# Attention by runs of two pairs of blocks, with TensorE in program order inside the loop

## The chip, the cores and the metric

The kernel runs on one core of one Trainium2 chip (trn2). The metric is the device time of one execution in microseconds. Other times are from one profiled execution of the kernel before.

## The reference

One hybrid decoder block over 2048 tokens of width 1024, batch 1, depth 1. One input projection gives an LRU branch, its gate, and q, k, v; a recurrence (RG-LRU) and a sliding-window attention run side by side; their normed outputs go through one output projection; a squared-ReLU MLP follows. What the change touches is the attention (16 query heads of 64, 2 key/value heads, blocks of 128 queries against the block before and their own, a learned sink in the denominator):

```python
def sliding_window_sink_attention(q, k, v, sinks):
    ...
    scores = jnp.einsum('bnqhgd,bnkhd->bnhgqk', qb, kwin).astype(jnp.float32) * scale
    ...
    mask = (kpos <= qpos) & (kpos > qpos - WINDOW) & (kpos >= 0)
    scores = jnp.where(mask[None, :, None, None], scores, NEG_INF)
    ...
    m = jnp.maximum(jnp.max(scores, axis=-1, keepdims=True), sink)
    p = jnp.exp(scores - m)
    denom = jnp.sum(p, axis=-1, keepdims=True) + jnp.exp(sink - m)
    probs = (p / denom).astype(v.dtype)
    out = jnp.einsum('bnhgqk,bnkhd->bnqhgd', probs, vwin)
```

## The kernel before

The sequence is worked in two halves of 1024 tokens (`c` = 0, 1; eight blocks of 128 each). A half goes through the norm and its transposes, the projections of k and v, the attention loop, the LRU, the output projection and the first MLP product; the second MLP product comes after both halves. Float32 factors are split into a high and a low part (`split_weight`, L157 to L168: `whi` on ScalarE at L166, `wlo` on VectorE at L167), so a projection is three matmuls (L224, L225, L227).

**The attention loop** (`for s in range(NH + 1)`, NH = 16 heads) is a software pipeline. Step `s` computes the scores of head `s`, the transposed probabilities of head `s - 1` and, four pairs later, the value products; beside them it runs pieces of a projection. It goes over four pairs of blocks, `p` = 0 to 3. What one pair issues:

- `Head.scores`: four matmuls (L584, tile `sc`) into one PSUM bank, two of which take turns; VectorE selects the window (L592, or L589 and L590 at the first pair of the first half), takes the maximum (L594) and scales it (L595); ScalarE does two exponentials into `st` (L598).
- `Head.probs`: two transposes (L614) into `tpb[:, p % 2]`; ScalarE copies them out as the high half of `pf` (L617), VectorE makes the low half (L618), GpSimd selects the two windows (L621, L623).
- `Head.values`: twelve matmuls of 64 columns (L638, tile `av`) from `pf`. Behind the fourth pair VectorE scales the head's result (L645, `yq`).
- `piece`: six matmuls of 512 columns, of the next q projection (`qps`), and near the end of the loop of the LRU's first inputs (`xps`, `gpps`). When a q projection is done, at the end of every even step, it is scaled and split: ScalarE L562 and VectorE L563, twice.
- `flip`, once in two heads: eight transposes (L655, `ytp`), ScalarE's copy L656 and square L662, VectorE's L665.

Both halves of `tpb` are one tile of 2 KB per partition, in one PSUM bank:

```python
tpb = bank(2, "tp", (P, 2, 2, P))
...
tp = tpb[:, p % 2]
```

**What sets the order.** The framework orders the instructions of each engine itself, by a priority heap over the traced program and a model of its own, and puts in the waits on semaphores. Each engine then issues its list strictly in that order. The change names TensorE as an engine whose list is the program's own, between two points.

Of the kernel before, what the change touches and what calls it, by code (L numbers as in the profile page):

```python
# [37 lines left out]
def hybrid_block_kernel(  # L38
# [16 lines left out]
    act = nc.scalar  # L55
    dve = nc.vector
    pe = nc.tensor
    chain = [None]

    def chained(ins):  # L60
# [24 lines left out]
    def U(i, name, dt=F32, shape=(P, D)):  # L85
        return S(f"u{i}", name, dt, shape)
# [400 lines left out]
    for c in range(NCH):  # L487
# [59 lines left out]
        def new_q(j):  # L547

            w = split_weight(w_in[16 + j])
            ps = mm("qps", j % 2)  # L550

            def piece(i):
                n, k = divmod(i, 4)
                proj_mm((ps[:, :HALF], ps[:, HALF:]), w, hn, (n,), (2 * k, 2 * k + 1))

            def done():

                qs = [U((16, 8, 9, 10)[(2 * j + hh) % 4], "qs", F32R) for hh in range(2)]
                for hh in range(2):
                    s_ = slice(hh * HD, hh * HD + HD)  # L560
                    o_ = slice((1 - hh) * HD, (1 - hh) * HD + HD)
                    act.activation(qs[hh][s_, :], ps[s_, :], AF.Copy, scale=0.125)  # L562
                    dve.scalar_tensor_tensor(out=qs[hh][o_, :], in0=ps[s_, :], scalar=0.125,  # L563
                                             in1=f32(qs[hh][s_, :]), op0=ALU.mult, op1=ALU.subtract)
                return qs
            return piece, done
# [83 lines left out]
        def flip(j, yq):  # L650

            yt = U(15, "yt")
            tp = mm("ytp", j % 2)
            for b in range(NT):
                pe.transpose(tp[:, b * P:(b + 1) * P], yq[:, b, :], ident)  # L655
            act.activation(yt, tp, AF.Copy, scale=usc[:, j // 4:j // 4 + 1])  # L656
            nc.gpsimd.dma_start(ydr[j], yt)
            if j == 0:
                act.activation(acca, yt, AF.Square)
            else:  # L660
                sq = yq.rearrange("p a b -> p (a b)")
                act.activation(sq, yt, AF.Square)  # L662
                for m in range(2):
                    hs = slice(m * HALF, (m + 1) * HALF)
                    dve.tensor_tensor(acca[:, hs], acca[:, hs], sq[:, hs], op=ALU.add)  # L665
# [77 lines left out]
        qs, yqs, heads = {}, {}, {}  # L743
        pf_next = [0]
        late = []
        piece, done = new_q(0)
# [3 lines left out]
        piece, done = new_q(1)  # L750
        for i in range(4):
            piece(i)
        lru_in = None
        for s in range(NH + 1):
            j = s // 2
            if s < NH:
                if s % 2 == 0:
                    yqs[j] = U(3 + j % 2, "yq", F32, (P, NT, P))
                heads[s] = Head(s, qs[j][s % 2], yqs[j])
            if s % 2 == 1:  # L760
                if j + 2 < KT:
                    piece, done = new_q(j + 2)
                else:
                    piece, done = (new_x if j + 2 == KT else new_gate)(0)
            for p in range(4):
                if s < NH:
                    heads[s].scores(p)
                    if p == 3:
                        heads[s].sums()
                if len(late) == 4:  # L770
                    for _ in range(2):
                        heads[late[0][0]].values(late.pop(0)[1])
                if s > 0:
                    heads[s - 1].probs(p)
                    late.append((s - 1, p))
                    if p == 3 and s % 2 == 1 and s > 1:
                        flip(j - 1, yqs[j - 1])
                piece(p if s % 2 else 4 + p)
            if s % 2 == 0:
                if j + 1 < KT:  # L780
                    qs[j + 1] = done()
                elif j + 1 == KT:
                    lru_in = done()
                else:
                    lru_in.append(done())
        for h, p in late:
            heads[h].values(p)
        flip(KT - 1, yqs[KT - 1])
# [450 lines left out]
```

## Time and profile before

| | |
|---|---|
| median of 3 runs | 2533.41 us (2530.89 to 2533.82) |
| the profiled execution | 2528.75 us |
| its span | 2527.0 us |
| TensorE busy in the span | 2427.9 us, 96% |
| VectorE, ScalarE, GpSimd | 70%, 50%, 19% |
| attention loop of the first half, first scores of head 0 to those of head 15 | 70.56 to 229.34 us |
| the same of the second half | 1000.16 to 1159.08 us |

A row of the timeline has the start, the time from the first start to the last end of the merged instructions, the engine, the source line and operation, the tiles (out<-in), the shapes and the count; in brackets the engine's idle time just before and what ended it. Matmuls overlap, so what one costs is read from start to start.

### The profile page before, as it was taken

What the parts mean: (1) busy time and instruction counts of PE and PEld (TensorE: products, weight loads), DVE (VectorE), ACT (ScalarE), POOL (GpSimd) and SP (SyncE); (2) the same over time, 40 slices, a digit from 0 to 9 for tenths busy, and PEclk for the clock granted to TensorE, in tenths of its full rate; (3) what the DMA queues carried; (4) which work ended last, traced back from release to release, by engine and by line L of the source; (5) the groups of instructions that cost most, each with busy time, mean ns of one, the idle gap of its engine ahead of it and who ended that gap; (6) DMA issues with size and microseconds to landing.
All of it is one profiled execution on the core that took longest, in us unless ns stands there. A gap on an engine that the chain in (4) does not pass through costs nothing.

```text
span 2527.0 us, 32551 instructions
## 1 busy us (share of the span) xinstructions
PE 2427.9 (96%) x12338; PEld 1981.7 (78%) x12338; DVE 1768.6 (70%) x2389; ACT 1253.8 (50%) x2084; POOL 481.7 (19%) x461
## 2 busy tenths in 40 slices
PE   7999999999999999999999998999989999999997
PEld 6887787787788877887778787788868777888885
DVE  6788566857655565876758748555575898887888
ACT  5666777414554465666778215454454233222334
POOL 0355000001333210554000011233230110111100
PEclk9999999999999999999999999999989999999999
DMA  4111112312344443111114212444453454443334
GB/s 154 43 51 43 53 45 101 120 50 105 112 151 156 147 167 117 42 48 51 45 44 141 101 42 92 146 146 154 150 200 117 154 162 156 134 136 119 127 103 148
DMA packets 133324, 276.37 MB, mean 109 GB/s; under 512 B 11184, under 2 KB 70576, under 8 KB 133168
## 3 DMA queue, kind: packets, MB, share of 16 engines
q1 hardware_dynamic: 125680, 248.08, 29.2%
q0 software_dynamic: 4608, 16.78, 1.8%
q10 hardware_dynamic: 2880, 9.44, 0.9%
q8 instruction: 97, 1.59, 0.2%
q14 instruction: 59, 0.48, 0.1%
HBM read 190.37 MB, written 83.89 MB: 109 GB/s over the span
## 4 chain that ended last, share of the span: by engine, by line
PE 63%; DVE 16%; issue 12%; ACT 7%; POOL 1%; DMA 1%; POOLq 0%; SPq 0%; DVEq 0%; ACTq 0%
PE ops L932 11%; PE dd L1149 10%; PE qr L394 10%; PE pa L394 9%; PE pb L394 3%; PE sc L584 2%; DVE acc L1158 2%; PE qps L224 2%; PE qps L227 2%; PE qps L225 2%; DVE xc L691 2%; PE xps L225 1%; PE xps L224 1%; PE xps L227 1%; PE av L638 1%
## 5 line engine op out<-in xcount | busy, mean ns | idle before, releaser
L1158 DVE TENSOR_TENSOR acc<-dd,acc 128x1024 f32<-128x1024 f32 x207 | 250.9, 1219 | 94.1 <-PE dd L1149 93.5
L932 PE MATMUL ops<-whi,ht 128*128 128x512 f32 x1024 | 277.6, 390 | 0.0
L962 ACT ACTIVATE ah<-araw 128x1024 fp32r<-128x1024 f32 x96 | 101.9, 1061 | 293.4 <-PE dd L1149 284.8
L932 PEld LDWEIGHTS ops<-whi,ht 128*128 128x128 f32 x1024 | 192.2, 188 | 40.7 <-DVE x L937 0.5
L932 PE MATMUL ops<-wlo,ht 128*128 128x512 f32 x512 | 159.7, 391 | 0.0
L372 POOL TENSOR_TENSOR s<-wraw 128x512 f32<-128x512 f32 x32 | 42.0, 1313 | 598.9 <-issue 327.8
L166 ACT ACTIVATE whi<-wraw 128x1024 fp32r<-128x1024 f32 x84 | 88.6, 1056 | 121.5 <-PE ops L932 92.6
L621 POOL TENSOR_SCALAR_AFFINE_SELECT pf<-pf 128x512 f16<-128x512 f16 x128 | 86.1, 673 | 315.3 <-DVE pf L618 314.7
L963 DVE TENSOR_TENSOR al<-araw,ah 128x1024 fp32r<-128x1024 f32 x96 | 123.1, 1284 | 11.6 <-ACT ah L962 11.5
L598 ACT ACTIVATE st<-sc,mx 128x128 f32<-128x128 f32 x256 | 91.6, 364 | 63.1 <-DVE mx L595 62.6
L167 DVE TENSOR_TENSOR wlo<-wraw,whi 128x1024 fp32r<-128x1024 f32 x82 | 104.4, 1278 | 25.5 <-issue 9.8
L932 PEld LDWEIGHTS ops<-wlo,ht 128*128 128x128 f32 x512 | 95.6, 188 | 20.5 <-DVE wlo L167 1.2
L224 PE MATMUL qps<-ht,whi 128*128 128x512 f32 x256 | 108.3, 423 | 0.0
L380 ACT ACTIVATE f2h<-wraw 128x1024 fp32r<-128x1024 f32 x32 | 34.0, 1061 | 142.9 <-DMA act<-hid 111.9
L394 PE MATMUL qr<-hm,s 128*128 128x512 f32 x384 | 100.3, 411 | 3.6 <-DVE hid L427 3.6
L225 PE MATMUL qps<-ht,whi 128*128 128x512 f32 x256 | 102.0, 398 | 0.0
L224 PE MATMUL xps<-ht,whi 128*128 128x512 f32 x256 | 101.5, 396 | 0.0
L227 PE MATMUL qps<-ht,wlo 128*128 128x512 f32 x256 | 101.2, 395 | 0.0
L225 PE MATMUL xps<-ht,whi 128*128 128x512 f32 x256 | 100.9, 394 | 0.0
L224 PE MATMUL gpps<-ht,whi 128*128 128x512 f32 x256 | 100.8, 394 | 0.0
L225 PE MATMUL gpps<-ht,whi 128*128 128x512 f32 x256 | 100.1, 391 | 0.0
L381 DVE TENSOR_TENSOR f2l<-wraw,f2h 128x1024 fp32r<-128x1024 f32 x32 | 39.2, 1224 | 79.4 <-ACT f2h L380 79.4
(324 smaller groups left out, 6899.6 us busy)
## 6 DMA issues: line engine op xcount, KB each, us to landing
araw<-act SPq DMA_DIRECT2D x96, 512.0 KB, 3.5
wraw<-in_w_up_dram SPq DMA_DIRECT2D x64, 512.0 KB, 3.2
act<-hid SPq DMA_DIRECT2D x128, 256.0 KB, 2.6
wraw<-in_w_in_dram SPq DMA_DIRECT2D x52, 512.0 KB, 3.2
act<-a SPq DMA_DIRECT2D x96, 256.0 KB, 2.4
wraw<-in_w_out_dram SPq DMA_DIRECT2D x32, 512.0 KB, 3.2
braw<-in_w_down_dram SPq DMA_DIRECT2D x32, 512.0 KB, 4.3
xt<-in_x_dram SPq DMA_DIRECT2D x16, 512.0 KB, 4.5
```

The source lines that it names most:

```text
L166: act.activation(hi, raw, AF.Copy)
L167: (eng or dve).tensor_tensor(lo, raw, f32(hi), op=ALU.subtract)
L224: pe.matmul(ps[m], w[0][:, k * P:(k + 1) * P], hk(ht[m][0], k), start=(k == 0), stop=False)
L225: pe.matmul(ps[m], w[0][:, k * P:(k + 1) * P], hk(ht[m][1], k), start=False, stop=False)
L227: pe.matmul(ps[m], w[1][:, k * P:(k + 1) * P], hk(ht[m][0], k), start=False, stop=(k == KT - 1))
L394: pe.matmul(ps, w[a_][:, ks], hk(h[b_], k), start=first and k == 0 and i == 0, stop=k == KT // 2 - 1 and i == 2, skip_group_check=True)
L598: ins = act.activation(self.st[:, b, :], cur[:, i, :], AF.Exp, bias=self.mx[:, b:b + 1], accum_out=self.ls[:, b:b + 1])
L932: pe.matmul(ps[m], a_, wk[k][b_][:, hs], start=(k == 0 and a_ is yh and b_ == 0), stop=(k == kn - 1 and a_ is ylo))
L962: act.activation(hi, raw, AF.Copy)
L963: dve.tensor_tensor(lo, raw, f32(hi), op=ALU.subtract)
L1149: pe.matmul(o[:, i, :], a_[:, t0:t0 + P], b_[:, r, :], start=first and r == 0 and k == 0, stop=r == 1 and k == 2, skip_group_check=True)
L1158: dve.tensor_tensor(accs[blk][d_], o, accs[blk][d_], op=ALU.add)
```

## The change

The loop body takes the four pairs in two runs (`p0` = 0 and 2). A run issues the scores of two pairs, then the value products of two pairs, then the transposes of two pairs, then two pieces of a projection. Around the loop, `tc.manual_schedule(engines={PE})` keeps TensorE's instructions in the order in which the program issues them; the other engines are ordered by the framework as before.

```diff
--- before.py
+++ after.py
@@ -55,6 +55,7 @@
     act = nc.scalar
     dve = nc.vector
     pe = nc.tensor
+    PE = mybir.EngineType.PE
     chain = [None]
 
     def chained(ins):
@@ -751,6 +752,8 @@
         for i in range(4):
             piece(i)
         lru_in = None
+        order = ctx.enter_context(ExitStack())
+        order.enter_context(tc.manual_schedule(engines={PE}))
         for s in range(NH + 1):
             j = s // 2
             if s < NH:
@@ -762,20 +765,24 @@
                     piece, done = new_q(j + 2)
                 else:
                     piece, done = (new_x if j + 2 == KT else new_gate)(0)
-            for p in range(4):
+
+            for p0 in (0, 2):
                 if s < NH:
-                    heads[s].scores(p)
-                    if p == 3:
+                    for p in (p0, p0 + 1):
+                        heads[s].scores(p)
+                    if p0:
                         heads[s].sums()
                 if len(late) == 4:
                     for _ in range(2):
                         heads[late[0][0]].values(late.pop(0)[1])
                 if s > 0:
-                    heads[s - 1].probs(p)
-                    late.append((s - 1, p))
-                    if p == 3 and s % 2 == 1 and s > 1:
+                    for p in (p0, p0 + 1):
+                        heads[s - 1].probs(p)
+                        late.append((s - 1, p))
+                    if p0 and s % 2 == 1 and s > 1:
                         flip(j - 1, yqs[j - 1])
-                piece(p if s % 2 else 4 + p)
+                for p in (p0, p0 + 1):
+                    piece(p if s % 2 else 4 + p)
             if s % 2 == 0:
                 if j + 1 < KT:
                     qs[j + 1] = done()
@@ -783,6 +790,7 @@
                     lru_in = done()
                 else:
                     lru_in.append(done())
+        order.close()
         for h, p in late:
             heads[h].values(p)
         flip(KT - 1, yqs[KT - 1])
```

Line numbers behind the inserted lines are one higher in the changed kernel up to the loop (L618 becomes L619, L614 becomes L615), and eight higher behind it.

TensorE at step 1, where the first transposes of the loop stand, in the kernel before (`kcar` and `kd` are keys, `tp` the transposes, `qps` the projection; the names in brackets are the semaphores waited for, DVE is VectorE):

```order
L584 MATMUL sc<-kcar,qs 128x256 [waits DVE_49,PE_49,Activation_49]
L584 MATMUL sc<-kcar,qs 128x256
L584 MATMUL sc<-kd,qs 128x256 x2
L614 MATMUL tp<-ident,st 128x128 x2
L224 MATMUL qps<-ht,whi 128x512
L225 MATMUL qps<-ht,whi 128x512
L227 MATMUL qps<-ht,wlo 128x512
L224 MATMUL qps<-ht,whi 128x512
L225 MATMUL qps<-ht,whi 128x512
L227 MATMUL qps<-ht,wlo 128x512
L584 MATMUL sc<-kd,qs 128x256 [waits DVE_49,PE_49,Activation_49]
L584 MATMUL sc<-kd,qs 128x256 x3
```

The same place in the changed kernel:

```order
L585 MATMUL sc<-kcar,qs 128x256 [waits DVE_49,PE_49,Activation_49]
L585 MATMUL sc<-kcar,qs 128x256
L585 MATMUL sc<-kd,qs 128x256 x2
L585 MATMUL sc<-kd,qs 128x256 [waits DVE_49,PE_49,Activation_49]
L585 MATMUL sc<-kd,qs 128x256 x3
L615 MATMUL tp<-ident,st 128x128 x2
L615 MATMUL tp<-ident,st 128x128 [waits DVE_49]
L615 MATMUL tp<-ident,st 128x128
L225 MATMUL qps<-ht,whi 128x512
L226 MATMUL qps<-ht,whi 128x512
L228 MATMUL qps<-ht,wlo 128x512
```

The first two transposes carry no wait in either; the next two, which stood behind projections and scores, now stand right behind the first two, with a wait for VectorE.

VectorE at the beginning of step 5, an odd step, in the kernel before (`wlo` is the low part of a weight, `mx` the maximum of scores, `pf` the transposed probabilities):

```order
L167 TENSOR_TENSOR wlo<-wraw,whi 128x1024
L606 TENSOR_TENSOR ls<-ls,es 128x8
L589 COPY_PREDICATED sc<-prevm,negt 128x128
L607 TENSOR_SCALAR ls<-ls 128x8
L590 COPY_PREDICATED sc<-prevm,sc 128x128
L608 RECIPROCAL ls<-ls 128x8
L594 TENSOR_REDUCE mx<-sc 128x2
L563 SCALAR_TENSOR_TENSOR qs<-qps,qs 64x1024
L595 TENSOR_SCALAR mx<-mx,snk 128x2
L618 SCALAR_TENSOR_TENSOR pf<-tp,pf 128x256
L592 COPY_PREDICATED sc<-prevm,sc 128x2x128
```

And in the changed kernel:

```order
L168 TENSOR_TENSOR wlo<-wraw,whi 128x1024
L590 COPY_PREDICATED sc<-prevm,negt 128x128
L564 SCALAR_TENSOR_TENSOR qs<-qps,qs 64x1024
L591 COPY_PREDICATED sc<-prevm,sc 128x128
L593 COPY_PREDICATED sc<-prevm,sc 128x2x128
L595 TENSOR_REDUCE mx<-sc 128x2 x2
L564 SCALAR_TENSOR_TENSOR qs<-qps,qs 64x1024
L596 TENSOR_SCALAR mx<-mx,snk 128x2 x2
L619 SCALAR_TENSOR_TENSOR pf<-tp,pf 128x256 x2
```

Before, one of the two `qs` operations stood ahead of the first `pf` of the step; now both do, and the work on two tiles of scores.

## Rows read from the trace of the kernel before

**Rows 1.** The page's first part: busy us, share of the span and instructions by engine

```profile
PE 2427.9 (96%) x12338; PEld 1981.7 (78%) x12338; DVE 1768.6 (70%) x2389; ACT 1253.8 (50%) x2084; POOL 481.7 (19%) x461
```

**Rows 2.** Stretches of the span: length, busy us and count by engine, clock, DMA

```profile
70.56:229.34 158.78, 153.37 (x1385) 130.49 (x1384) 128.14 (x338) 101.27 (x342) 76.74 (x117) 1.00 0.12 44
```

**Rows 3.** TensorE's timeline, two pairs of blocks in step 2

```profile
91.95 0.64 PE L584 MATMUL sc<-kd,qs 128*128 128x256 f32 x4
92.43 0.26 PE L638 MATMUL av<-vpa,pf 128*128 128x64 f16 x3
...
93.14 0.42 PE L614 MATMUL tp<-ident,st 128*128 128x128 f32 x2
93.31 0.48 PE L224 MATMUL qps<-ht,whi 128*128 128x512 f32 x1
93.63 0.39 PE L225 MATMUL qps<-ht,whi 128*128 128x512 f32 x1
...
94.79 0.64 PE L584 MATMUL sc<-kd,qs 128*128 128x256 f32 x4
...
96.88 0.40 PE L584 MATMUL sc<-kcar,qs 128*128 128x256 f32 x2
```

**Rows 4.** TensorE's timeline: first scores of head 13 and of head 15

```profile
207.23 0.40 PE L584 MATMUL sc<-kcar,qs 128*128 128x256 f32 x2
...
229.34 0.40 PE L584 MATMUL sc<-kcar,qs 128*128 128x256 f32 x2
```

**Rows 5.** Timeline of all engines, beginning of step 3

```profile
98.07 0.41 PE L614 MATMUL tp<-ident,st 128*128 128x128 f32 x2
...
101.39 0.42 DVE L618 SCALAR_TENSOR_TENSOR pf<-tp,pf 128x256 f16<-128x256 f32 x1
101.73 0.42 DVE L592 COPY_PREDICATED sc<-prevm,sc 128x256 f32<-128x256 uint32 x1
101.86 0.44 PE L614 MATMUL tp<-ident,st 128*128 128x128 f32 x2 [0.81 <-DVE pf L618]
```

**Rows 6.** TensorE's waits, 70 to 260 us: total us, times, longest

```profile
PE tp L614 <- DVE pf L618: 5.9, 8, 0.8
```

**Rows 7.** Timeline of all engines, step 14

```profile
223.00 0.44 PE L614 MATMUL tp<-ident,st 128*128 128x128 f32 x2
...
223.94 0.42 DVE L618 SCALAR_TENSOR_TENSOR pf<-tp,pf 128x256 f16<-128x256 f32 x1 [0.16 <-ACT pf L617]
...
224.44 0.63 PE L584 MATMUL sc<-kd,qs 128*128 128x256 f32 x4
...
225.11 0.43 DVE L592 COPY_PREDICATED sc<-prevm,sc 128x256 f32<-128x256 uint32 x1 [0.60 <-PE sc L584]
```

**Rows 8.** Groups by line and shape, 95 to 215 us: count, busy us, mean ns

```profile
L594 DVE TENSOR_REDUCE mx<-sc 128x2 f32<-128x256 f32 x43 | 18.2, 423 | 0.9
L563 DVE SCALAR_TENSOR_TENSOR qs<-qps,qs 64x1024 fp32r<-64x1024 f32 x12 | 14.7, 1222 | 0.4
L167 DVE TENSOR_TENSOR wlo<-wraw,whi 128x1024 fp32r<-128x1024 f32 x6 | 9.7, 1623 | 0.1
L595 DVE TENSOR_SCALAR mx<-mx,snk 128x2 f32<-128x2 f32 x43 | 9.5, 221 | 0.4
L645 DVE TENSOR_TENSOR yq<-av,ls 128x512 f32<-128x512 f32 x10 | 6.8, 682 | 0.0
```

**Rows 9.** TensorE's timeline at two holes

```profile
463.50 1.09 PE L673 MATMUL sqt<-ident,accq 128*128 128x128 f32 x8 [1.70 <-POOL accq L873]
...
1883.24 0.99 PE L394 MATMUL qr<-hm,s 128*128 128x512 f32 x3 [1.75 <-DVE hid L427]
```

**Rows 10.** Stretches around these holes: TensorE's busy us and count, granted clock, DMA

```profile
461.00:464.00 3.00, 1.30 (x8) 1.00 0.97 380
...
1884.02:1887.43 3.41, 3.41 (x9) 0.50 0.00 0
1887.43:1890.00 2.57, 2.57 (x13) 1.00 0.68 208
```

## Prediction

> **What bounds the kernel now.** I read the busy shares first, then the two attention loops by stretches, then TensorE's timeline inside them, then its waits. TensorE is busy for 96% of the span and no other engine comes near [rows 1]. In the first of the two loops (one for each half of the sequence) it is busy 153.4 of 158.8 us at a granted clock of 1.00 [rows 2]. So the loop is a stream of TensorE work with small holes, and every microsecond by which TensorE stands still there is added to the end: the stages behind it wait for TensorE's results, and it is just as full in them.
>
> What a step costs is in the timeline [rows 3]. Two pairs of blocks take 96.88 - 91.95 = **4.93 us**: four scores 0.48, 24 value products 0.71, the two transposes of a pair 0.17 up to the next projection, six projections 1.48, and the second pair again without value products. Two steps (two heads) take 229.34 - 207.23 = **22.1 us** [rows 4]. Four times 4.93 is 19.7. The other 2.4 are the eight transposes of `flip`, 0.7 to 0.9 at the rate of [rows 3], and holes.
>
> The holes have one cause [rows 5, 6]. The transposes of a pair at 101.86 start 0.05 us after the L618 that began at 101.39 has ended, and this L618 is the one that empties the pair transposed at 98.07. So a pair waits until the pair right before it has been read out of PSUM, although the two use different halves of `tpb`: both halves lie in one bank. The kernel before pays 5.9 us for this in the whole first loop, because six projections and four scores stand between two pairs of transposes.
>
> The Trainium skill says under "Perfetto Trace Analysis", section Matmuls, that independent groups should rotate through different PSUM banks, so that emptying one overlaps the next. By that rule this change brings together what should be apart; with two banks it would end at the time of rival D below, with one bank, as the row at 101.86 has it, at my forecast.
>
> **The change, part by part.** (1) Scores, value products and projections are the same instructions in the same number. Merged runs save almost nothing: the first projection behind a pair of transposes takes 0.32 to the next one, the others 0.23 [rows 3], so 0.09 for each second pair, and the transposes inside a run of four lose about as much, since nothing overlaps the end of the first two. I set this at 0.
>
> (2) **The second pair of transposes now follows the first directly.** The order shows the wait: in the first run of the loop the first two transposes carry none, the next two wait for VectorE. Nothing but L619 (L618 before) of the first pair can be meant there. Since TensorE now goes in program order, the twelve projections of the run and the next scores stand behind this wait; before, six projections ran in that time. The price of one wait is read where VectorE and ScalarE were free [rows 7]: transposes at 223.00, ScalarE's copy, L618 from 223.94 to 224.36, and 0.05 more: 1.41 from first transpose to the next pair. A plain run is then 0.96 (eight scores) + 0.71 + 1.41 + 0.17 + 1.48 + 6 x 0.23 = **6.1 us** in place of 4.93, so +1.2.
>
> (3) In the second run of each step VectorE has L645 (L646 now, 0.68 us, [rows 8]) queued ahead of that L618. Its scores' work begins 0.67 after the first of four scores [rows 7]; for the second four that is 0.48 + 0.67 = 1.15 into the run. Behind it come two reductions and two small operations, which brings L645 to about 2.4 and the end of L618 to about 3.45, where the plain run has 3.03. So +0.4, between 0 and 0.68: **6.5 us**.
>
> (4) In the first run of every odd step VectorE's order has much more ahead of L618: the weight's low part (1.62), both L563 (1.22 each), two predicated copies (0.43 each), two reductions (0.42), two L595 (0.22), then L618 (0.42) [rows 5, 7, 8]: 6.6 us from the end of the projections, which is where the run's scores begin. Neighbours overlap at their ends (L592 starts 0.34 after a L618 that takes 0.42 [rows 5]), nine times some 0.08, so about 5.9. Before, one L563 stood behind L618 and the hole there was 0.81 [rows 5]. The second pair starts at 5.9 into the run and the rest is again 3.05: **8.95 us**, +4.0; the bounds are +3.4 (if the weight's part runs partly before the projections end) and +4.7 (no overlap).
>
> Two steps: 6.1 + 6.5 + 8.95 + 6.5 + 0.9 for `flip` = 29.0 against 22.1, **+6.9**. There are eight such pairs of steps in a loop. The first has no transposes in its step 0, the last has the convolution's operations on VectorE where the others have L563; I take them as equal to the rest. 8 x 6.9 = 55 for a loop, **110 us for both**.
>
> (5) **TensorE's clock.** Behind a hole of 1.75 us between matmuls of 512 columns the clock was granted at 0.50, which is 1.2 GHz, for 3.41 us; 9 matmuls ran in that stretch, and 13 in the 2.57 us at 1.00 (2.4 GHz) after it [rows 9, 10]. Such a fall costs up to 3.41 x (1 - 0.20/0.38) = 1.6 us. Behind a hole of 1.70 the clock stayed at 1.00 [rows 9, 10]. The waits of part 4 leave TensorE idle for some 4 us, twice these holes, so I expect a fall behind each: 16 of them, at 1.45 since some of the stretch falls into the hole, **23 us**. The waits of part 2, 1.1 us, are shorter than either hole; those of part 3, about 1.5, are nearly as long, and I count none.
>
> (6) Hidden: ScalarE's and GpSimd's work for a run (VectorE's 69% share and ScalarE's 50% over the span [rows 1]) has more time than before; the value products take what was selected two runs earlier. If a wait appeared there it would lie inside the longer run.
>
> Sum: the profiled execution took 2528.75 us, its span 2527.0; + 110 + 23 gives 2662. The median of the runs, 2533.41, is 4.7 above that execution, so the forecast is **2666 us**.
>
> **Rivals.** B: the waits are there, but the clock stays up through them. For it: the hole of 1.70 that cost no clock; against: the one of 1.75 that did, when the holes of part 4 are twice that. Time 2533 + 110 = 2643. C: the clock falls behind the 32 waits of part 3 too, at 1.45 each, 46 more: 2712. For it: they are about as long as the hole of 1.75; against: the 24 value products stand just before them. D, the other side: the second pair needn't wait for the first but only for its own half of the bank, so that runs of two pairs leave no hole, and the holes of the old order go. The place is the second transposes of a run, the price 5.9 in each loop [rows 6], the point at which it decides is whether those transposes start within 0.2 us of the first ones or more than 1 us later. 2533 - 12 = 2521. Against it stand the 0.81 behind the neighbour's L618 [rows 5] and the wait in the order. E: TensorE's order does not become the program's, or what it loses in the loop is given back behind it because the next stage waits for VectorE or ScalarE anyway: 2533. The order excludes the first; the second would need a stage in which TensorE is not full.
>
> **How the numbers follow.** Forecast 0.62, B 0.20, C 0.12, D 0.04, E 0.02. 0.2% (5 us) is about what a measurement of this kernel can tell from none. A change of the forecast, B or C is far above it, so slower 0.94, same 0.02, faster 0.04. The range: lowest, every run pays only the plain 1.2 us, 64 x 1.2 = 77 less the 12 to 15 of holes that are in the old time, no clock lost: 2595; highest, case C: 2715. This leaves out D and E and little else.
>
> **What would show it.** Right: L615 waits for L619 in each of the 32 runs of a loop that have transposes, 1.1 us at least and about 4 us once in two steps; two steps take 29 us; the granted clock drops below 1.00 within the loops; the stages behind are as long as before. Wrong: the transposes of a run stand together without idle time (D), the loop's clock stays at 1.00 (B), or the loop is longer by 110 and the span is not (E).

## The result and the profile after

The changed kernel takes **2673.4 us** (median, 2671.48 to 2674.81) where the kernel before takes 2532.6 beside it (2530.89 to 2533.82). The ratio is 1.0559, with a 95% interval of 1.0545 to 1.0572. The forecast was 2666 us, with a range of 2595 to 2715. The profiled execution took 2671.48 us, its span is 2669.8.

TensorE's share of the span falls from 96% [rows 1] to 92%; the busy time rises by 27 us, with instructions that last longer at the lower clock (below). First part of the page of the changed kernel:

```profile
PE 2454.9 (92%) x12338; PEld 2001.1 (75%) x12338; DVE 1763.5 (66%) x2389; ACT 1250.7 (47%) x2084; POOL 464.8 (17%) x461
```

Next, TensorE's timeline over steps 8 and 9 of the first loop, an even and an odd one: two steps, four runs, to be held against the two steps of [rows 4]. (L615 is L614 of before, L619 is L618.)

```profile
188.47 0.40 PE L585 MATMUL sc<-kcar,qs 128*128 128x256 f32 x2
...
190.14 0.42 PE L615 MATMUL tp<-ident,st 128*128 128x128 f32 x2
191.63 0.44 PE L615 MATMUL tp<-ident,st 128*128 128x128 f32 x2 [1.08 <-DVE pf L619]
...
194.68 1.11 PE L585 MATMUL sc<-kd,qs 128*128 128x256 f32 x8
...
198.16 0.44 PE L615 MATMUL tp<-ident,st 128*128 128x128 f32 x2 [1.40 <-DVE pf L619]
...
201.21 0.40 PE L585 MATMUL sc<-kcar,qs 128*128 128x256 f32 x2
...
207.35 0.44 PE L615 MATMUL tp<-ident,st 128*128 128x128 f32 x2 [4.06 <-DVE pf L619]
...
211.96 1.11 PE L585 MATMUL sc<-kd,qs 128*128 128x256 f32 x8
...
215.44 0.44 PE L615 MATMUL tp<-ident,st 128*128 128x128 f32 x2 [1.40 <-DVE pf L619]
...
219.35 0.40 PE L585 MATMUL sc<-kcar,qs 128*128 128x256 f32 x2
```

Each of these runs has a hole in front of its second pair of transposes; so have 29 of the first loop's 32 runs with transposes, all but the last three. The plain run takes 194.68 - 188.47 = 6.21 us, the second run of the step 6.53, the first of the odd step 10.75, its second, with `flip`, 7.39. Together 30.88, where before two steps took 22.1 [rows 4]: +8.8.

What fills the 4.06 is on VectorE, same stretch:

```profile
201.18 1.23 DVE L168 TENSOR_TENSOR wlo<-wraw,whi 128x1024 fp32r<-128x1024 f32 x1 [1.12 <-PE qps L226]
202.32 0.29 DVE L590 COPY_PREDICATED sc<-prevm,negt 128x128 f32<-128x128 uint32 x1
202.65 1.22 DVE L564 SCALAR_TENSOR_TENSOR qs<-qps,qs 64x1024 fp32r<-64x1024 f32 x1
...
204.43 0.76 DVE L595 TENSOR_REDUCE mx<-sc 128x2 f32<-128x256 f32 x2
205.22 1.23 DVE L564 SCALAR_TENSOR_TENSOR qs<-qps,qs 64x1024 fp32r<-64x1024 f32 x1
206.48 0.36 DVE L596 TENSOR_SCALAR mx<-mx,snk 128x2 f32<-128x2 f32 x2
206.87 0.42 DVE L619 SCALAR_TENSOR_TENSOR pf<-tp,pf 128x256 f16<-128x256 f32 x1
```

VectorE is never idle from 201.18 to the end of that L619 at 207.29, and the transposes follow 0.06 later. Two groups of TensorE's waits in the first loop (70 to 320 us; total, times, longest), in place of [rows 6]:

```profile
PE tp L615 <- DVE pf L619: 63.0, 29, 6.6
PE gpps L225 <- ACT st L599: 1.2, 1, 1.2
```

And stretches of the span (length; busy us and count of TensorE, its weight loads, VectorE, ScalarE and GpSimd; granted clock; DMA): one behind a 4.06 hole, one up to the next such hole, and each loop from the first scores of head 0 to those of head 15.

```profile
146.55:149.97 3.42, 3.42 (x9) 2.67 (x8) 0.42 (x1) 0.24 (x1) 1.59 (x3) 0.50 0.00 0
149.97:177.27 27.30, 19.36 (x193) 16.54 (x192) 17.52 (x46) 13.89 (x49) 8.58 (x15) 1.00 0.11 40
70.69:293.73 223.04, 166.59 (x1386) 140.39 (x1384) 126.58 (x341) 99.19 (x346) 71.70 (x118) 0.93 0.09 32
1071.34:1294.09 222.75, 166.49 (x1386) 140.28 (x1384) 125.64 (x326) 101.13 (x345) 71.55 (x118) 0.94 0.09 32
```

The first loop's stretch is 223.04 - 158.78 [rows 2] = 64.3 us longer. The same stretch of the second loop grew by as much, and what remains of the span's 142.8 us lies in the loops' last steps, where the wait of 6.6 stands. The stages behind the loops give nothing back: from the transposes that follow the first loop (tile `sqt`) to the second loop's first scores it is 739.2 us, where before it was 739.1.

### The profile page after: what moved, and what is told of

It reads as the page before. It is cut to its first block, busy times and chain, and to the rows that moved or that the text cites. A ratio compares the mean times of both kernels' runs of the same rounds, so it can differ in the third digit from the quotient of the medians.

```text
span 2669.8 us, 32592 instructions
## 1 busy us (share of the span) xinstructions
PE 2454.9 (92%) x12338; PEld 2001.1 (75%) x12338; DVE 1763.5 (66%) x2389; ACT 1250.7 (47%) x2084; POOL 464.8 (17%) x461
## 3 DMA queue, kind: packets, MB, share of 16 engines
q8 instruction: 97, 1.59, 0.2%
## 4 chain that ended last, share of the span: by engine, by line
PE 60%; DVE 19%; issue 12%; ACT 7%; DMA 1%; POOL 1%; POOLq 0%; SPq 0%; DVEq 0%; ACTq 0%
PE ops L940 11%; PE qr L395 10%; PE dd L1157 10%; PE pa L395 9%; PE pb L395 3%; PE qps L225 2%; PE qps L226 2%; PE qps L228 2%; DVE acc L1166 2%; DVE xc L692 1%; DVE mx L595 1%; PE sc L585 1%; PE xps L226 1%; PE xps L225 1%; DVE qs L564 1%
## 5 line engine op out<-in xcount | busy, mean ns | idle before, releaser
L615 PE MATMUL tp<-ident,st 128*128 128x128 f32 x256 | 57.0, 306 | 123.5 <-DVE pf L619 123.5
L618 ACT ACTIVATE pf<-tp 128x256 f16<-128x256 f32 x128 | 49.8, 389 | 201.4 <-PE tp L615 184.6
L168 DVE TENSOR_TENSOR wlo<-wraw,whi 128x1024 fp32r<-128x1024 f32 x82 | 100.0, 1226 | 46.6 <-PE qps L226 17.4
L615 PEld LDWEIGHTS tp<-ident,st 128*128 128x128 f32 x256 | 27.1, 146 | 138.3 <-DVE pf L619 137.8
L593 DVE COPY_PREDICATED sc<-prevm,sc 128x256 f32<-128x256 uint32 x112 | 47.2, 426 | 101.4 <-PE sc L585 99.8
L225 PE MATMUL qps<-ht,whi 128*128 128x512 f32 x256 | 113.6, 444 | 0.0
L226 PE MATMUL qps<-ht,whi 128*128 128x512 f32 x256 | 107.8, 421 | 0.0
L228 PE MATMUL qps<-ht,wlo 128*128 128x512 f32 x256 | 107.5, 420 | 0.0
L225 PE MATMUL gpps<-ht,whi 128*128 128x512 f32 x256 | 102.6, 401 | 2.5 <-ACT st L599 2.5
L599 ACT ACTIVATE st<-sc,mx 128x128 f32<-128x128 f32 x256 | 90.6, 368 | 30.4 <-DVE mx L596 29.5
L226 PE MATMUL xps<-ht,whi 128*128 128x512 f32 x256 | 101.6, 397 | 0.0
```

The costliest lines, as they stand in the source:

```text
L168: (eng or dve).tensor_tensor(lo, raw, f32(hi), op=ALU.subtract)
L225: pe.matmul(ps[m], w[0][:, k * P:(k + 1) * P], hk(ht[m][0], k), start=(k == 0), stop=False)
L226: pe.matmul(ps[m], w[0][:, k * P:(k + 1) * P], hk(ht[m][1], k), start=False, stop=False)
L228: pe.matmul(ps[m], w[1][:, k * P:(k + 1) * P], hk(ht[m][0], k), start=False, stop=(k == KT - 1))
L599: ins = act.activation(self.st[:, b, :], cur[:, i, :], AF.Exp, bias=self.mx[:, b:b + 1], accum_out=self.ls[:, b:b + 1])
```

## Which half of the change costs: order alone, runs alone

The change joins two things, and each was run without the other. First, the old single pairs in program order on TensorE:

```diff
+        order.enter_context(tc.manual_schedule(engines={PE}))
         for s in range(NH + 1):
...
             for p in range(4):
```

> The old loop of single pairs, with TensorE in program order. Part of the change by itself. My theory: six projections and four scores stand between two pairs of transposes as before, so the waits stay as small as in the kernel before (5.9 us in a loop) and the time is that of the kernel before within 10 us, 2523 to 2545. Rival (program order is what costs, because TensorE can no longer be given other work while VectorE is late): 2640 to 2680.

Measured: **2547.7 us** (2544.95 to 2548.89), ratio 1.0054 [1.0039, 1.0069]. That is 14 us above the kernel before and 3 above the theory's upper end, and far from the rival. The timeline of TensorE shows what is left: in the odd steps one pair still waits, behind one L564 in VectorE's queue, and longer than the 0.81 of [rows 5]. The waits for L619 in the first loop are 15.3 us in place of 5.9 [rows 6]; 4.0 of them are one wait at the loop's end.

```profile
170.65 0.44 PE L615 MATMUL tp<-ident,st 128*128 128x128 f32 x2 [1.53 <-DVE pf L619]
```

Second, the runs of two pairs with TensorE's order left to the scheduler (the line of program order taken out):

```diff
-        order.enter_context(tc.manual_schedule(engines={PE}))
```

> The runs of two pairs with TensorE's instructions placed by the scheduler, the other part of the change by itself. TensorE's order here has projections or scores between the two pairs of transposes of most runs. My theory: the loss goes to the extent that they stand apart, 2530 to 2565 us. Rival (grouping scores and value products in twos costs by itself, since VectorE gets two pairs' work at once): above 2620.

Measured: **2532.9 us** (2531.65 to 2534.77), ratio 0.9998 [0.9989, 1.0008]: no difference. Its waits in the first loop are those of the kernel before:

```profile
PE tp L615 <- DVE pf L619: 6.4, 9, 1.4
```

So neither half costs much: +14 and 0 where both together cost 141. The loss is in what they make jointly, the two pairs of transposes side by side with nothing allowed in between.

## The place of the second pair of transposes

Runs and program order stay; only the first pair's six projections go between the two pairs again:

```diff
-                if s > 0:
-                    for p in (p0, p0 + 1):
+                for p in (p0, p0 + 1):
+                    if s > 0:
                         heads[s - 1].probs(p)
...
-                for p in (p0, p0 + 1):
                     piece(p if s % 2 else 4 + p)
```

> Runs of two scores and two value products stay, and so does program order on TensorE; only the second pair's transposes are moved behind the first pair's six projections. My theory (the second pair stands too near the first pair's readout in the same bank): in a plain run the hole of 1.08 us is covered by 1.48 us of projections and goes; in the first run of an odd step the hole of 4.06 us shrinks by 1.5 to about 2.6, so the clock may still fall there once in two steps. Time 2570 to 2600 us. Rival 1 (grouping or program order itself costs, not the place of the second pair): as the changed kernel, 2665 to 2680. Rival 2 (the changed kernel's loss is nearly all in the odd steps' first runs and not in the 1.1 us waits): 16 x (4.06 - 2.6) = 23 us gained and no more, about 2650.

Measured: **2596.7 us** (2594.32 to 2597.52), ratio 1.0248 [1.0233, 1.0263]: 77 us of the 141 are gone, within the theory's range and outside both rivals. The first loop's waits for L619 fall by half, to 31.6 us, and on TensorE's timeline the hole of a plain run is covered in steps 2 and 4 (no idle time ahead of 121.43). From step 6 on 0.54 us of it is left (146.58), with the additions of `flip` (L666, two in 1.29 us) in VectorE's queue ahead of L619. The hole of an odd step stays:

```profile
119.79 0.41 PE L615 MATMUL tp<-ident,st 128*128 128x128 f32 x2
121.43 0.38 PE L615 MATMUL tp<-ident,st 128*128 128x128 f32 x2
...
128.19 0.40 PE L585 MATMUL sc<-kcar,qs 128*128 128x256 f32 x2
...
134.88 0.44 PE L615 MATMUL tp<-ident,st 128*128 128x128 f32 x2 [3.22 <-DVE pf L619]
...
146.58 0.44 PE L615 MATMUL tp<-ident,st 128*128 128x128 f32 x2 [0.54 <-DVE pf L619]
```

In the odd step 3.22 is left, where I expected 2.6: the pair starts 6.69 us into its run (134.88 - 128.19), 0.55 later than in the changed kernel, so the projections cover only part of it. Most of the 0.55 is L590, which took 0.73 us beside a select of GpSimd where it took 0.29 in the changed kernel.

The other way is to give the second pair nothing in its own run to wait for. All four transposes go ahead of both readouts:

```diff
+            def turn(self, p):
+                for i in range(2):
+                    pe.transpose(tpb[:, p % 2, i, :], self.st[:, 2 * p + i, :], ident)
...
                 if s > 0:
+                    for p in (p0, p0 + 1):
+                        heads[s - 1].turn(p)
                     for p in (p0, p0 + 1):
                         heads[s - 1].probs(p)
```

> The changed kernel with all four transposes of a run ahead of the readouts of both pairs, so that the second pair has no readout of its own run to wait for; only the first pair of a run waits, for the readout of the run before, with twelve projections and eight scores in between. My theory (the wait for the readout in the same run is the whole loss): no hole inside a run, the clock stays up in the loop, 2515 to 2545 us. If instead VectorE's late work in odd steps only comes to be waited for elsewhere (scores of the next run, or its value products), part of the 4 us waits stays: 2545 to 2590. Rival (the four transposes wait for each other or the readouts of one bank hold the next run's scores up): above 2640.

Measured: **2568.7 us** (2567.66 to 2570.14), ratio 1.0139 [1.0124, 1.0154]: the second of the three cases. An odd step of it on TensorE:

```profile
175.04 0.63 PE L613 MATMUL tp<-ident,st 128*128 128x128 f32 x4
...
180.68 1.21 PE L585 MATMUL sc<-kd,qs 128*128 128x256 f32 x8 [2.23 <-ACT st L599]
...
182.44 0.64 PE L613 MATMUL tp<-ident,st 128*128 128x128 f32 x4
184.06 1.09 PE L658 MATMUL ytp<-ident,yq 128*128 128x128 f32 x8 [0.98 <-DVE yq L648]
```

The four transposes stand in one block of 0.63 us. The even steps take 9.8 us (163.58 to 173.38 by the first scores), 4.9 a run, which is the old price of two pairs [rows 3]. The odd steps from step 3 on take 14.4 to 14.9 (13.5 to 14.5 in the second loop), and they wait elsewhere: VectorE's long queue makes the row maxima (L596) late, with them the exponentials (L599), and the next scores wait for a score bank. ScalarE's timeline in the same step:

```profile
179.47 0.37 ACT L599 ACTIVATE st<-sc,mx 128x128 f32<-128x128 f32 x1 [2.25 <-DVE mx L596]
```

One wait is removed and two take its place, 2.23 and 0.98 us instead of 4.06 and 1.40.

## VectorE's queue in the odd steps

The forecast's part 4 says that the hole of the odd step is the sum of what VectorE has queued ahead of L619. Two runs take operations out of that queue in the changed kernel. In the first, the next query weight is split in the even step, and the second query half is made behind the first readouts:

```diff
+                if p0 == 0 and s % 2 == 0 and j + 2 < KT:
+                    wn = split_weight(w_in[16 + j + 2])
+                if p0 == 0 and s % 2 and j + 1 < KT:
+                    rest((1,))
...
-                    qs[j + 1] = done()
+                    qs[j + 1] = done((0,))
```

> The changed kernel with the same spreading of VectorE's work and nothing else: my part 4 and 5 by themselves. Of the operations ahead of L619 in the first run of an odd step the weight's low part and one query half go, 2.4 us: the second pair should start at about 3.7 us into the run in place of 6.1, the hole falls from 4.06 to about 1.7, the clock stays at 1.00 there. 16 x (2.4 + 1.56) = 63 us less than the changed kernel: 2600 to 2625. Rival 1 (the clock falls also behind holes of 1.7): 2630 to 2640. Rival 2 (the 4 us holes are not VectorE's queue): 2665 to 2680.

Measured: **2636.8 us** (2636.05 to 2637.37), ratio 1.0414 [1.04, 1.0428]: 37 us gained, not 48 to 73. The time alone falls into the range of rival 1, but its condition did not come about: the holes are 2.55 us in the first loop, not 1.7. VectorE's timeline in the first run of an odd step, whose scores begin at 191.13 (L621 and L617 are L619 and L615 there):

```profile
191.11 1.23 DVE L168 TENSOR_TENSOR wlo<-wraw,whi 128x1024 fp32r<-128x1024 f32 x1 [1.11 <-PE qps L226]
...
192.58 1.22 DVE L566 SCALAR_TENSOR_TENSOR qs<-qps,qs 64x1024 fp32r<-64x1024 f32 x1
...
195.29 0.42 DVE L621 SCALAR_TENSOR_TENSOR pf<-tp,pf 128x256 f16<-128x256 f32 x1
195.74 1.23 DVE L566 SCALAR_TENSOR_TENSOR qs<-qps,qs 64x1024 fp32r<-64x1024 f32 x1
```

TensorE's timeline of the same kernel, the second pair of transposes in this odd step and in an earlier one:

```profile
168.02 0.44 PE L617 MATMUL tp<-ident,st 128*128 128x128 f32 x2 [2.54 <-DVE pf L621]
...
195.76 0.44 PE L617 MATMUL tp<-ident,st 128*128 128x128 f32 x2 [2.55 <-DVE pf L621]
```

My edit did half of what its expectation says. The second L566 went behind L621. The weight's low part did not leave: it waits for the last projection that reads its buffer (the L226 in its row), which ends as the odd step begins, and the scheduler put a later weight's part there. One operation of 1.2 us out, the hole shorter by 4.06 - 2.55 = 1.5: what VectorE has queued between the run's scores and L619 sets the hole.

In the second run the low part of the query weights is made on GpSimd:

```diff
-            w = split_weight(w_in[16 + j])
+            w = split_weight(w_in[16 + j], eng=nc.gpsimd)
```

> The changed kernel with the low part of the query weights made on GpSimd in place of VectorE. My theory of part 4 (each operation of VectorE ahead of L619 in the first run of an odd step adds its time to the hole): the 1.2 us of that operation go from the hole of 4.06, which leaves 2.8. In the runs with the spread work a hole of 2.55 was followed by the fall of the clock in about half of the odd steps, so the fall stays in most. 16 x 1.2 = 19, and up to 10 of clock: 2644 to 2656 us. Rival (the hole is set by the two query halves and their high parts on ScalarE, not by the sum): 2665 to 2678. If GpSimd is slower at it than the wait allows, projections or value products wait for GpSimd: above 2680.

Measured: **2666.1 us** (2664.5 to 2670.12), ratio 1.0535 [1.0521, 1.055]; by the time alone, the rival. The trace tells more. GpSimd's timeline in the first run of an odd step of the first loop:

```profile
204.64 2.39 POOL L168 TENSOR_TENSOR wlo<-wraw,whi 128x1024 fp32r<-128x1024 f32 x1
```

VectorE's at the same time:

```profile
205.29 1.90 DVE L590 COPY_PREDICATED sc<-prevm,negt 128x128 f32<-128x128 uint32 x1 [1.83 <-PE sc L585]
```

TensorE's, the second pair of transposes in that step, and in an odd step of the second loop:

```profile
212.04 0.69 PE L615 MATMUL tp<-ident,st 128*128 128x128 f32 x2 [5.35 <-DVE pf L619]
...
1153.71 0.44 PE L615 MATMUL tp<-ident,st 128*128 128x128 f32 x2 [2.19 <-DVE pf L619]
```

L590 takes 1.90 in place of 0.29 us: it overlaps GpSimd's subtraction and ends 0.16 after it, and the hole grew to 5.35 (in step 7, where the second L564 went behind L619, it was 3.71). In the second loop the step has no L590 (it is issued only for the first half of the sequence), GpSimd's L168 stands at the same place, and the hole is 2.19 where the changed kernel has 3.99. Two things differ there. VectorE has no L168, and the scheduler put the second L564 behind L619, where in the changed kernel it stands ahead:

```profile
1150.12 0.91 DVE L593 COPY_PREDICATED sc<-prevm,sc 128x256 f32<-128x256 uint32 x2 [1.81 <-PE sc L585]
...
1153.23 0.42 DVE L619 SCALAR_TENSOR_TENSOR pf<-tp,pf 128x256 f16<-128x256 f32 x1
1153.68 1.23 DVE L564 SCALAR_TENSOR_TENSOR qs<-qps,qs 64x1024 fp32r<-64x1024 f32 x1
```

The step's scores begin at 1149.44, and VectorE, idle, waits for them until 0.68 us later. In the changed kernel, with L168 ahead, it began 1.12 us after the scores (1141.97 and 1140.85). So only 0.44 of L168's 1.23 us lengthened the hole; the rest of the 1.80 comes with the second L564. My theory that L168 adds its whole time was wrong, and the rival, the two query halves, has the larger part.

The edit also reached only five of a loop's eight odd steps, and I had counted 16 in both: from step 11 on L168 is of another projection's weight and stays on VectorE, and the holes there are as in the changed kernel. From head 0 to head 15 the second loop is 12 us shorter than in the changed kernel (210.6 against 222.75), the first is 4.5 longer (227.5 against 223.04), and 5 more are lost between them.

The Trainium skill, "SBUF — State Buffer", section "Who interferes with whom", has a rule for this: a VectorE instruction with two inputs in SBUF contends with a GpSimd instruction that reads SBUF, through a port pair that works as an exclusive lock. The trace agrees: L590 reads mask and data from SBUF and was held (1.90), while L593, whose data comes from PSUM, was not (0.91 for two beside the L168 of the second loop).

As a control, the same spreading in the kernel before, where only 5.9 us of such waits are in the first loop [rows 6]:

> Control: the kernel before with the same spreading of VectorE's work. There only 5.9 us of waits for VectorE stand in the first loop. My theory: at most these and a few more for both loops, 2522 to 2534 us. If it gains as much as the same edit on the changed kernel (60 us) then the spreading removes something else than the waits named.

Measured: **2531.5 us** (2528.04 to 2533.79), ratio 0.9999 [0.999, 1.0008]. The 5.9 us of waits are still there, and the edit gains nothing.

## Towards a version that beats both

The spreading on top of the four transposes first:

> The kernel with the four transposes first, and VectorE's work of the odd steps spread: the next weight's high and low part are made in the even step before, and of the two query halves the second is made behind the first readouts of the odd step. My theory: the kernel with the transposes first loses only in odd steps, 14.4 us where the even ones take 9.8, and there because 1.2 (weight) + 1.2 (second half) of VectorE stand ahead of the reductions on which the exponentials and with them the next scores wait. Without these 2.4 us the odd step takes 10.6 (9.8 and the eight transposes of flip), up to 12 if some wait is left: 16 x 2.4 to 3.8, so 2508 to 2530 us from 2569, and at or below the kernel before. Rival (the scores wait because the exponentials of a run's second pair come late on ScalarE, whatever VectorE does): 2555 to 2575.

Measured: **2546.3 us** (2544.48 to 2547.58), ratio 1.0055 [1.0041, 1.0069]: 22 us gained of 39 to 61, between the theory's range and the rival's. One wait for exponentials is down to 0.72, since half of the edit was void as above, and `flip` still waits 0.98 for L650 (L646 of the changed kernel), which I had left out. An odd step on TensorE:

```profile
173.10 1.22 PE L587 MATMUL sc<-kd,qs 128*128 128x256 f32 x8 [0.72 <-ACT st L601]
...
176.48 1.09 PE L660 MATMUL ytp<-ident,yq 128*128 128x128 f32 x8 [0.98 <-DVE yq L650]
```

So `flip` was moved behind the twelve projections of its run:

```diff
-                    if p0 and s % 2 == 1 and s > 1:
-                        flip(j - 1, yqs[j - 1])
                 for p in (p0, p0 + 1):
                     piece(p if s % 2 else 4 + p)
+                if p0 and s % 2 == 1 and s > 1:
+                    flip(j - 1, yqs[j - 1])
```

> The kernel with the transposes first, the work spread and program order, with flip's transposes moved behind the run's twelve projections. My theory: in the odd steps 0.98 us of waiting for the scaled values (L650) goes, 14 times: 2546 less 14 is 2532, between 2528 and 2537. What is left against the free order is the loop's end and 0.7 us waits for exponentials. Rival (the wait only moves to the next run's scores): 2542 to 2550.

Measured: **2535.3 us** (2533.74 to 2537.56), ratio 1.0014 [1.0005, 1.0023], within the range: the wait of `flip` is gone, 11 us gained where I expected 14.

Then the kernel with four transposes first and the work spread, `flip` at its old place, with program order given up:

```diff
-        order.enter_context(tc.manual_schedule(engines={PE}))
```

> The kernel with the transposes first and the work spread, with TensorE's order left to the scheduler, which keeps the four transposes together and puts three to six projections between the groups. If program order costs at the ends of the loop (late work of the last heads not filled in), this is some 5 to 10 us faster than the same kernel in program order: 2500 to 2520. If the scheduler puts scores where VectorE isn't ready: 2520 to 2545.

Measured: **2516.9 us** (2516.17 to 2519.89), ratio 0.9944 [0.9932, 0.9957]. This is faster than both kernels, by 14.7 us against the one before. The first loop, from the first scores of head 0 to those of head 15, takes 155.23 us in place of 158.78 [rows 2], with TensorE busy for 152.49 of it; the second takes 152.44 in place of 158.92.

```profile
70.65:225.88 155.23, 152.49 (x1386) 131.51 (x1384) 121.36 (x337) 99.13 (x346) 76.40 (x116) 1.00 0.13 45
```

The time is in the expected range, the reason only in part: giving up program order gained 29 us, not 5 to 10, and 8.4 and 9.1 of it lie inside these two stretches (163.62 and 161.56 us in program order), not at the ends of the loops.

Whether the spreading is needed for it was asked by leaving it out:

> Four transposes first, TensorE's order left to the scheduler, VectorE's work not spread. It tells what made the last one of the runs (2516.9 us) faster than the kernel before. If the place of the transposes and the free order are enough: 2512 to 2522. If the spreading was needed, because a run's scores wait for the exponentials in odd steps: 2525 to 2545.

Measured: **2535.1 us** (2532.67 to 2537.42), ratio 1.0013 [1.0005, 1.0022]. It is: without it scores wait 10.0 us for exponentials in the first loop, with it 3.6. Neither part gains alone (0.9999 and 1.0013); together they do. Whether the transposes have to stand first for it is open: runs of two pairs in the scheduler's order with the work spread, but the transposes as in the change, were not run. Last, the weight's low part on GpSimd in that version:

> The kernel with four transposes first, the work spread and TensorE's order free (2516.9 us), with the low part of the query weights on GpSimd. VectorE gains 1.2 us in each odd step; waits for exponentials were 3.6 us in the first loop. My theory: 3 to 8 us less, 2508 to 2515. Rival (TensorE is the bound there already): 2515 to 2519. If GpSimd's selects come late: above 2520.

Measured: **2531.9 us** (2528.63 to 2533.49), ratio 1.0000 [0.9991, 1.0009]: 15 us worse, in the range of the third case but not for its reason, since the value products wait no longer for GpSimd's selects than without the edit (0.7 us in the first loop). In its first loop the copy with `negt` is held again (1.90 us at 143.13, beside GpSimd's subtraction from 142.48 to 144.87), and scores wait 10.1.

## Why the prediction was right, point by point

**What bounds** the kernel held: TensorE in the loop. The 141 us came out at the end undiminished, and rival E (given back behind the loop) fell. Two readings were slightly off, without weight in the sum: VectorE's share is 70% [rows 1], not 69, and the holes of the kernel before had a second cause, 1.4 us of waits for GpSimd's selects in the stretch of [rows 6].

**Part 1** (merged runs save nothing): the runs alone, 0.9998, don't contradict it.

**Part 2**, a plain run at 6.1: measured 6.21, hole 1.08. Over the loops the shortest holes are 0.98. That the second pair waits for the first pair's readout is shown by the two runs that take that neighbour away, one with projections in between and one with the transposes ahead of the readout. That the common bank is the reason, rather than the common tile, is not shown: no run gives the two pairs a bank each. Rival D (no wait) fell with the row at 191.63. The rule of the Trainium skill ("Perfetto Trace Analysis", section Matmuls) that the prediction set against the change agrees with the trace on the side that was run, groups in one bank: 1.08 us is the shortest hole in this stretch.

**Part 3**, 6.5 for the second run: 6.53, hole 1.40. The mechanism is the one named, VectorE's L646 ahead of L619:

```profile
197.09 0.69 DVE L646 TENSOR_TENSOR yq<-av,ls 128x512 f32<-128x512 f32 x1
197.69 0.41 DVE L619 SCALAR_TENSOR_TENSOR pf<-tp,pf 128x256 f16<-128x256 f32 x1
```

No clock was lost behind these in the stretch 149.97 to 177.27, at 1.00, which holds two of them; so rival C fell.

**Part 4**, the second pair of an odd step at 5.9 into the run: 207.35 - 201.21 = 6.14. The mechanism is the one named. That its size came out so close is partly luck, since errors in it nearly cancel. I took the weight's part at 1.62 [rows 8], and it measured 1.23. I counted two predicated copies at 0.43, and there are three (0.29, 0.28 and 0.41, two of them left out above). I took off 0.7 for overlaps; the operations, the reductions and L596 at 0.42 and 0.22 each, make 6.36 us and took 6.11, so that 0.25 was to be had. And the weight's part belongs to the sum only because the sum begins with the run's scores: taken out, it shortened the wait by 0.44 (second loop of the kernel with L168 on GpSimd).

**Part 5**, the clock: it fell to 0.50 (1.2 GHz) 16 times in the two loops, as forecast, each time at the first run of an odd step, and rival B fell. Eleven of these stretches lasted 3.4 us; five lasted 6.8, in steps 1 and 15 of both loops and step 3 of the first, which I had not expected. The rest of the run behind the hole took 211.96 - 207.35 = 4.61 where the plain run has 194.68 - 191.63 = 3.05: 1.56 for a fall, against my 1.45. The spread kernel gives this price a second time, from two odd steps with the same hole (2.54 and 2.55), one without and one with a fall:

```profile
163.40:178.45 15.05, 11.11 (x106) 9.53 (x104) 10.35 (x25) 9.85 (x28) 5.40 (x10) 1.00 0.10 35
191.13:207.77 16.64, 12.69 (x106) 10.69 (x104) 10.36 (x25) 9.56 (x26) 5.43 (x10) 0.90 0.10 32
```

16.64 - 15.05 = 1.59.

**Part 6** (other engines hidden) held: the waits of the first loop name nothing but L619, and once ScalarE for 1.2 us.

**The sum** was 9.5 us short of the profiled execution (2662 against 2671.48), and 7 of the median, since the 4.7 that I added for the median were 1.9. Two steps were put at 29.0 and 1.45 of clock, 30.45; they took 30.88 in the first loop, nearly all of the difference in the odd step's first run (10.75 instead of 10.4), and 30.62 in the second (1158.83 to 1189.45). 8 x 0.43 + 8 x 0.17 makes 5. The rest lies at the edges of the loops, where I took every pair of steps to be like the others, 6.9 + 1.45 = 8.35 each. Steps 1 and 2 took 10.9 us more than before in the first loop and 11.7 in the second (29.82 and 30.50 in place of 18.90 and 18.81), with longer holes and the low clock for longer; what follows the first scores of head 15, though the hole of 6.6 is there, took only 6.8 and 7.8 more. Step 1 of the first loop on TensorE, and the stretch at the low clock there:

```profile
84.48 0.69 PE L615 MATMUL tp<-ident,st 128*128 128x128 f32 x2 [5.02 <-DVE pf L619]
```

```profile
81.70:88.53 6.83, 4.05 (x11) 3.28 (x12) 3.06 (x7) 2.68 (x10) 2.45 (x4) 0.50 0.03 11
```

## What to carry to other kernels

When two groups share a PSUM bank, count what stands between one group and the readout of the other, not the slots: here six 512-column matmuls put back between them covered a wait of 1.1 us in plain runs, wholly or by half, shortened the long ones, and returned 77 of the 141 us. With a fixed program order an engine has nothing else to do while it waits for a late operation of another, so look at the queue ahead of the operation waited for, in the worst step of the pattern, before pinning the order. An operation at the head of that queue may cost less than its time, when the engine would have stood idle there anyway: 0.44 of 1.23 us here. A removed wait shows the next one: transposes first and VectorE's work spread gained nothing on the kernel before singly, 0.6% together, and only with the scheduler's order.

## What the runs showed that I had not expected

A hole's length alone did not decide whether the clock fell behind it. Of the twelve odd steps 3 to 13 of both loops, it fell in all twelve of the changed kernel (holes of 4.06 and 3.99), in five of the spread one (2.55 and 2.35, as in the two rows above), and in eight of the one with the second pair apart (3.2 and 2.7). With the four transposes first, it fell in two of the first loop's six (2.23). The prediction had argued from 1.70 against 1.75 [rows 9] as if a length between them were the border; and the hole of 1.75 was no clean example, since it began 0.9 us after a stretch of 10.2 us at 0.50 (1870.37 to 1880.61 in the kernel before). What decides between two equal holes stays open; no run was made for it.

GpSimd's subtraction of 128x1024 took 2.39 us where VectorE's took 1.23, and a VectorE copy beside it took 1.6 us longer: moving an operation to an engine that is busy for 17% of the span gained 7 us in the changed kernel and lost 15 in the fastest.
